# First stage of a two-layer decoder trunk: own buffers for all its loads, issued in a written order, first weights in halves

## Chip, cores and metric

One core of a Trainium2 chip runs the whole program. The metric is device microseconds of one execution; the program of before took 1174.53 us as the median of three runs (1172.65 to 1175.73).

## What is computed

A decoder trunk over 512 tokens of width 1024 with two layers, batch 1, all inputs float32. Layer 0 is a gated DeltaNet mixer beside a cross-attention into 256 memory tokens, layer 1 a sliding-window attention beside the same kind of memory attention; each has a squared-ReLU MLP and layer norms. Cut to what the first stage of the kernel feeds:

```python
def memory_cross_attention(qm, mem, w_kv):      # both layers, mem is an input
    kv = mem @ w_kv
    k = kv[..., :MEM_W]; v = kv[..., MEM_W:]    # MEM_W = 256
    ...

def mixer_a(h, mem, w_in, ...):                 # layer 0, h = x
    proj = h @ w_in
    qkv = proj[..., :c1]
    z = proj[..., c1:c1 + DN_V_W]
    a = proj[..., c1 + DN_V_W:c1 + DN_V_W + DN_HEADS]
    b = proj[..., c1 + DN_V_W + DN_HEADS:c1 + DN_V_W + 2 * DN_HEADS]
    qm = proj[..., c1 + DN_V_W + 2 * DN_HEADS:]
    beta = jax.nn.sigmoid(b); g = -jnp.exp(A_log) * jax.nn.softplus(a + dt_bias)
    o = gated_delta_rule(q, k, v, g, beta)
    ...
```

## The kernel before

Every float32 matrix is split into a high part (a cast to fp32r on ScalarE, ACT) and a low part (the rest, a subtraction on VectorE, DVE), and each product takes three matmuls: high times high, high times low, low times high. `wload` (L81) does this for weights: a raw buffer `wr` of a pool with three of them, one DMA from the queue of SyncE (SP), the cast into `wh` (L87), the subtraction into `wl` (L88); `wh` and `wl` have four buffers each. `split_load` (L192) does it for the transposed activations, with six raw buffers `xr`, in two halves of 256 KB.

The first stage is the memory keys and values of both layers (L205 to L220). `MH` and `ML` are the halves of the memory tokens; for layer i = 0, 1 the values `VM` come first (two weight slabs `wmv`, two groups of 24 matmuls of 256 columns), then the keys `KM` (two slabs `wmk`, two groups of 24 matmuls of 256 columns). So there are 8 groups of 24 matmuls. The second memory block is loaded behind the first weight slab (L210). Then come the loads of the four token blocks of x into `XH` and `XL` (L221), eight small loads (convolution weights, gate constants, positions, L223 to L231), and the stores of the keys and values of layer 1 to DRAM (`kv1`, L232 and L233), from where layer 1 reads them back far later (L1042). The tiles of this stage lie in the pool `mp`, which closes at L234; the pool `dp` of the mixer then takes its place, so a first write to a `dp` tile waits for whatever used that memory.

Behind it stands the first projection, `proj_z(2, ab)` (L255): two slabs of `wz`, four token blocks, 24 matmuls of 260 columns each, 96 in all; it gives the last z columns and the 12 gate columns `ab`. The gates are worked out from `ab` by a chain of small operations on DVE and ACT (L258 to L298). The memory queries `qm` and the keys and queries `kq` of the heads follow on TensorE (PE), by the hand-written list `MIXER_ORDER`.

A scheduler sets the order of each engine's instructions from the program's order and the dependencies; each engine then works strictly in that order. On the SP queue a load into a buffer that is still in use waits there, with all loads behind it. The weight loads use these lines:

```python
    wpool = [None, 3, 4]
        raw = wp.tile(shape, F32, tag="wr", name=nm("wr"), bufs=wpool[1])
        SY.dma_start(raw, src)
        hi = wp.tile(shape, F32R, tag="wh", name=nm("wh"), bufs=wpool[2])
```

Of the kernel before, what the change touches and what calls it, by code (L numbers as in the profile page):

```python
# [11 lines left out]
F32 = mybir.dt.float32  # L12
F32R = mybir.dt.float32r
# [5 lines left out]
P = 128  # L19
S = 512  # L20
D = 1024
NT = S // P
KT = D // P
NH = 6
CW = 260
# [24 lines left out]
def trunk(ctx: ExitStack, tc: tile.TileContext, xT, xn, memT, wk, wq, wv, wqm, wz, wmk, wmv, wo0, wo1, up, dn,  # L50
          bw, ws, conv, alog, dtb, nw, sinks, lng, lnb, lngb, pos, invf, out):
    nc = tc.nc
    V, G, A, T, SY = nc.vector, nc.gpsimd, nc.scalar, nc.tensor, nc.sync
# [8 lines left out]
    def nm(s):  # L62
        uid[0] += 1
        return f"{s}_{uid[0]}"

    def ct(shape, tag, dt=F32):
        return cp.tile(shape, dt, tag=tag, name=tag)

    def mmt(n="mm"):
        return pmm.tile([P, 512], F32, tag="mm", name=nm(n))  # L70

    def smt(n="sm"):
        return psm.tile([P, 512], F32, tag="sm", name=nm(n))

    def fr(ap):
        return ap.bitcast(F32)


    wpool = [None, 3, 4]

    def wload(src, shape):  # L81
        wp = wpool[0]
# [3 lines that stand above are left out]
        lo = wp.tile(shape, F32R, tag="wl", name=nm("wl"), bufs=wpool[2])  # L86
        A.copy(hi, raw)  # L87
        V.tensor_sub(lo, raw, fr(hi))  # L88
        return hi, lo
# [3 lines left out]
    XH = ct([P, KT, S], "XH", F32R)  # L93
    XL = ct([P, KT, S], "XL", F32R)
# [6 lines left out]
    def feature_major(ps, w, mov_hi, mov_lo):  # L101
        hi, lo = w
        for k in range(KT):
            mh, ml = mov_hi(k), mov_lo(k)
            T.matmul(ps, hi[:, k, :], mh, start=(k == 0), stop=False)
            T.matmul(ps, hi[:, k, :], ml, start=False, stop=False)
            T.matmul(ps, lo[:, k, :], mh, start=False, stop=(k == KT - 1))

    def token_major(ps, slabs, st_hi, st_lo):
        nk = sum(h.shape[1] for h, _ in slabs)  # L110
        k = 0
        for hi, lo in slabs:
            for kk in range(hi.shape[1]):
                sh, sl = st_hi(k), st_lo(k)
                T.matmul(ps, sh, hi[:, kk, :], start=(k == 0), stop=False)  # L115
                T.matmul(ps, sh, lo[:, kk, :], start=False, stop=False)  # L116
                T.matmul(ps, sl, hi[:, kk, :], start=False, stop=(k == nk - 1))  # L117
                k += 1
# [19 lines left out]
    def tok(t):  # L138
        return slice(t * P, (t + 1) * P)
# [4 lines left out]
    def x_tok(buf, t):  # L144
        return lambda k: buf[:, k, tok(t)]


    pa = ExitStack()
    km0 = pa.enter_context(tc.tile_pool(name="km0", bufs=1, side="right"))

    def c0(shape, tag, dt=F32):

        return km0.tile(shape, dt, tag=tag, name=tag)
# [31 lines left out]
    mpool = ctx.enter_context(ExitStack())  # L185
    mp = mpool.enter_context(tc.tile_pool(name="mp", bufs=1, side="right"))
    KM = [km0.tile([P, 2, 256], F32, tag="KM0", name="KM0"), mp.tile([P, 2, 256], F32, tag="KM1", name="KM1")]
    VM = [km0.tile([P, 2, 256], F32, tag="VM0", name="VM0"), mp.tile([P, 2, 256], F32, tag="VM1", name="VM1")]
    kv1 = drp.tile([2, P, 512], F32, tag="kv1", name="kv1", bufs=1)
    MH = mp.tile([P, 2, KT, P], F32R, tag="MH", name="MH")  # L190
    ML = mp.tile([P, 2, KT, P], F32R, tag="ML", name="ML")
    def split_load(src, hi, lo):  # L192
        raw = mp.tile([P, KT, P], F32, tag="xr", name=nm("xr"), bufs=6)
        for j in (slice(0, 4), slice(4, 8)):
            SY.dma_start(raw[:, j], src[:, j])
        for j in (slice(0, 4), slice(4, 8)):
            A.copy(hi[:, j], raw[:, j])
            V.tensor_sub(lo[:, j], raw[:, j], fr(hi[:, j]))

    warm_in = mp.tile([P, P], F32, tag="warm_in", name="warm_in")  # L200
    V.memset(warm_in, 1.0)
    warm = smt("warm")
    for i in range(14):
        T.matmul(warm[:, 0:P], warm_in, warm_in, start=True, stop=True)
    split_load(memT[0], MH[:, 0], ML[:, 0])  # L205
    for i in range(2):
        slabs = []
        for kh in range(2):
            slabs.append(wload(wmv[i, kh], [P, 4, 256]))
            if i == 0 and kh == 0:  # L210
                split_load(memT[1], MH[:, 1], ML[:, 1])
        for m in range(2):
            ps = mmt("VM")
            token_major(ps[:, :256], slabs, lambda k: MH[:, m, k, :], lambda k: ML[:, m, k, :])
            A.copy(VM[i][:, m, :], ps[:, :256])
        for j in range(2):
            w = wload(wmk[i, j], [P, KT, P])
            ps = mmt("KM")
            feature_major(ps[:, :256], w, lambda k: MH[:, :, k, :], lambda k: ML[:, :, k, :])
            A.copy(KM[i][:, j, :], ps[:, :256])  # L220
    for t in range(NT):  # L221
        split_load(xT[t], XH[:, :, tok(t)], XL[:, :, tok(t)])
    SY.dma_start(convw, conv)  # L223
    SY.dma_start(gbT, lngb)
    alog_b = row_bcast(alog, NH, "alog_b")
# [3 lines left out]
    invf_b = row_bcast(invf, 32, "invf_b")  # L229
    pos_i = ct([P, NT], "pos_i", I32)  # L230
    SY.dma_start(pos_i, pos)  # L231
    SY.dma_start(kv1[0], KM[1].rearrange("p a b -> p (a b)"))  # L232
    SY.dma_start(kv1[1], VM[1].rearrange("p a b -> p (a b)"))  # L233
    mpool.close()  # L234


    dp = pa.enter_context(tc.tile_pool(name="dp", bufs=2, side="right"))

    def dt_(shape, tag, bufs=2, dt=F32):
        return dp.tile(shape, dt, tag=tag, name=nm(tag), bufs=bufs)  # L240

    def proj_z(zg, gates=None):

        slabs = [wload(wz[zg, kh], [P, 4, CW]) for kh in range(2)]
        c0 = zg * CW
        n = min(CW, 768 - c0)
        for t in range(NT):
            ps = mmt("proj_zMM")
            token_major(ps[:, :CW], slabs, x_tok(XH, t), x_tok(XL, t))
            A.copy(res[:, t, c0:c0 + n], ps[:, :n])  # L250
            if gates is not None:
                V.tensor_copy(gates[:, :, t], ps[:, n:n + 12])

    ab = c0([P, 12, NT], "ab")
    proj_z(2, ab)  # L255


    gg = [c0([P, 24], f"gate{i}") for i in range(12)]  # L258
# [34 lines left out]
    ps = smt("v6ps")  # L293
# [10 lines left out]
    def make_E1(gi):  # L304
        E1 = dt_([P, NU, P], "E1")
        for hl in range(GH):
            h = GH * gi + hl
            ps = smt("E1")
            psv = ps.rearrange("p (c i) -> p c i", c=4)
            for i, eng in enumerate((V, G)):  # L310
                gm = dt_([P, 4, P], "y", dt=F32R)
                eng.tensor_tensor(gm, triu[:, :].unsqueeze(1).broadcast_to([P, 4, P]),
                                  fr(gsp[i])[:, h * 4:h * 4 + 4].unsqueeze(2).broadcast_to([P, 4, P]), op=ALU.mult)
                T.matmul(ps, slow, gm.rearrange("p c i -> p (c i)"), start=(i == 0), stop=(i == 1))
            dst = E1[:, hl * 4:hl * 4 + 4, :]
            V.tensor_tensor(dst, psv, mtri[:, :].unsqueeze(1).broadcast_to([P, 4, P]), op=ALU.add)
            A.activation(dst, dst, AF.Exp)
        E1s[gi] = E1

    def conv_silu(ps, ch, dst):  # L320
        y = dt_([P, 512], "y")
        A.activation(y, ps, AF.Identity, scale=convw[:, ch, 3:4])
        for s in (1, 2, 3):
            V.scalar_tensor_tensor(y[:, s:], ps[:, :512 - s], convw[:, ch, 3 - s:4 - s], y[:, s:],
                                   op0=ALU.mult, op1=ALU.add)
        A.activation(dst, y.rearrange("p (c i) -> p c i", c=4), AF.Silu)
# [415 lines left out]
    def second_pools():  # L742
# [7 lines left out]

    steps = {"E": make_E1, "g": group_open, "k": group_kq, "i": inv_blocks, "j": inv_join, "v": group_v,
             "w": group_v2, "c": group_chunk, "o": chunk_out, "q": proj_qm, "m": mem0, "M": flush, "z": proj_z,
             "n": z_norm, "W": wo_open, "f": close_tile, "p": wo_tile, "X": second_pools, "L": ln_tile}
    run_steps(MIXER_ORDER, steps)
# [281 lines left out]
    with tc.tile_pool(name="l1", bufs=2) as lp:  # L1036
# [155 lines left out]
        slabs = {}  # L1192
# [89 lines left out]
```

## Time and profile before

| | us |
|---|---|
| median of three runs | 1174.53 (1172.65 to 1175.73) |
| the profiled execution, its own time | 1170.9 |
| its span | 1169.2 |
| PE busy | 1137.7 (97%) |
| DVE, ACT, POOL busy | 860.7, 555.8, 242.5 |
| granted clock of PE, mean of the span | 0.992 of full speed |

The span is the profiled execution from its first to its last instruction; 1.7 us lie around it. A granted clock of 1.00 is the level of 2.4 GHz, 0.50 that of 1.2 GHz. Where one engine is busy nearly all the time, the time of the kernel is that engine's work, its rate, and the stretches in which it waits.

### The profile page before, as it was taken

The numbers are of one execution on the slowest core, as the hardware profiler recorded it, in microseconds if no ns is written. First come the engines' busy times: TensorE is split into PE (matmuls) and PEld (weight loads), VectorE is DVE, ScalarE is ACT, GpSimd is POOL, SyncE is SP. The second block draws the span as 40 slices with busy tenths as digits, with TensorE's granted clock in tenths as the row PEclk, the third lists the DMA queues.
The fourth block names the chain that finished last, engine by engine and source line by source line (L and its number), as shares of the span: only waits on it lengthen the run. The fifth ranks groups of instructions, "written<-read, shape, count | busy, mean of one in ns | idle before, by whom it ended". The sixth has DMA issues, their size and how long they took to land.

```text
span 1169.2 us, 18962 instructions
## 1 busy us (share of the span) xinstructions
PE 1137.7 (97%) x7470; PEld 1000.1 (86%) x7470; DVE 860.7 (74%) x1606; ACT 555.8 (48%) x1010; POOL 242.5 (21%) x180
## 2 busy tenths in 40 slices
PE   8999999999999999999999999999999999999996
PEld 8877788879998989898998887778989998989985
DVE  5568899777798666667665968986987666676657
ACT  6345454655385434444443337562655344444431
POOL 1112111101005232423220100000042324242204
PEclk9999999999999999999999999999999999999998
DMA  7522141203413324232332242102333242323311
GB/s 257 194 63 77 61 137 37 68 20 105 166 57 127 124 75 139 76 125 92 100 117 92 71 129 71 54 21 72 109 118 118 77 140 73 126 91 105 112 37 72
DMA packets 40729, 114.16 MB, mean 98 GB/s; under 512 B 11136, under 2 KB 12032, under 8 KB 40640
## 3 DMA queue, kind: packets, MB, share of 16 engines
q1 hardware_dynamic: 40064, 112.04, 29.8%
q8 instruction: 58, 0.95, 0.3%
q10 hardware_dynamic: 576, 0.92, 0.2%
q14 instruction: 31, 0.25, 0.1%
HBM read 109.53 MB, written 3.41 MB: 97 GB/s over the span
## 4 chain that ended last, share of the span: by engine, by line
PE 76%; DVE 15%; ACT 3%; DMA 2%; issue 2%; POOL 1%; POOLq 0%; SPq 0%; ACTq 0%; DVEq 0%
PE dn L116 9%; PE dn L117 9%; PE dn L115 9%; PE upb L884 3%; PE upb L885 3%; PE upb L886 3%; PE wo L117 2%; DVE wl L88 2%; PE wo L115 2%; PE wo L116 2%; PE upd L885 2%; PE upd L884 2%; PE upd L886 2%; PE upa L885 2%; PE upa L884 2%; PE upa L886 2%
## 5 line engine op out<-in xcount | busy, mean ns | idle before, releaser
L87 ACT CAST wh<-wr 128x1024 fp32r<-128x1024 f32 (+1 forms) x136 | 142.6, 1052 | 221.9 <-PE dn L117 154.6
L88 DVE TENSOR_TENSOR wl<-wr,wh 128x1024 fp32r<-128x1024 f32 (+1 forms) x136 | 166.3, 1225 | 77.7 <-ACT wh L87 77.0
L115 PE MATMUL dn<-wh,hh 128*128 128x512 f32 x512 | 199.5, 390 | 0.0
L117 PE MATMUL dn<-wh,hl 128*128 128x512 f32 x512 | 199.4, 389 | 0.0
L116 PE MATMUL dn<-wl,hh 128*128 128x512 f32 x512 | 199.4, 389 | 0.0
L117 PEld LDWEIGHTS dn<-wh,hl 128*128 128x128 f32 x512 | 96.1, 188 | 20.1
L963 DVE TENSOR_TENSOR res<-res,dn 128x512 f32<-128x512 f32 x120 | 81.8, 682 | 42.4 <-PE dn L117 42.3
L116 PEld LDWEIGHTS dn<-wl,hh 128*128 128x128 f32 x512 | 96.1, 188 | 19.1
L115 PEld LDWEIGHTS dn<-wh,hh 128*128 128x128 f32 x512 | 96.1, 188 | 19.0
L874 POOL TENSOR_TENSOR sa<-wr 128x512 f32<-128x512 f32 x26 | 39.0, 1500 | 351.0 <-DMA wr<-in_up_dram 311.1
L662 POOL TENSOR_TENSOR rs<-rs,nhalf 128x1 f32<-128x1 f32 x16 | 13.3, 833 | 327.2 <-DVE rs L661 264.0
L884 PE MATMUL upb<-TH,wh 128*128 128x256 f32 x208 | 57.5, 277 | 1.5 <-DVE u L923 1.5
L885 PE MATMUL upa<-XL,wh 128*128 128x256 f32 x208 | 57.7, 277 | 0.0
L886 PE MATMUL upa<-XH,wl 128*128 128x256 f32 x208 | 57.5, 276 | 0.0
L122 DVE TENSOR_TENSOR hl<-r,hh 128x1024 fp32r<-128x1024 f32 x26 | 56.1, 2156 | 1.9 <-ACT hh L121 1.9
L885 PE MATMUL upb<-TL,wh 128*128 128x256 f32 x208 | 57.4, 276 | 0.0
L886 PE MATMUL upb<-TH,wl 128*128 128x256 f32 x208 | 57.4, 276 | 0.0
L884 PE MATMUL upd<-XH,wh 128*128 128x256 f32 x208 | 57.4, 276 | 0.0
L885 PE MATMUL upd<-XL,wh 128*128 128x256 f32 x208 | 57.4, 276 | 0.0
L886 PE MATMUL upd<-XH,wl 128*128 128x256 f32 x208 | 57.4, 276 | 0.0
L875 POOL TENSOR_TENSOR sb<-sa,wr 128x512 f32<-128x512 f32 x26 | 57.4, 2207 | 0.0
L121 ACT CAST wh<-wr 128x1024 fp32r<-128x1024 f32 x26 | 27.4, 1053 | 53.5 <-PE upa L885 53.5
(405 smaller groups left out, 3296.8 us busy)
## 6 DMA issues: line engine op xcount, KB each, us to landing
wr<-in_up_dram SPq DMA_DIRECT2D x64, 512.0 KB, 4.3
wr<-in_dn_dram SPq DMA_DIRECT2D x64, 512.0 KB, 4.3
wr<-in_wo_dram SPq DMA_DIRECT2D x16, 512.0 KB, 3.6
wr<-in_bw_dram SPq DMA_DIRECT2D x8, 512.0 KB, 4.5
wr<-in_wz_dram SPq DMA_DIRECT2D x6, 520.0 KB, 4.4
wr<-in_wk_dram SPq DMA_DIRECT2D x6, 512.0 KB, 3.6
wr<-in_wq_dram SPq DMA_DIRECT2D x6, 512.0 KB, 3.7
wr<-in_wv_dram SPq DMA_DIRECT2D x6, 512.0 KB, 3.6
```

The source lines that it names most:

```text
L87: A.copy(hi, raw)
L88: V.tensor_sub(lo, raw, fr(hi))
L115: T.matmul(ps, sh, hi[:, kk, :], start=(k == 0), stop=False)
L116: T.matmul(ps, sh, lo[:, kk, :], start=False, stop=False)
L117: T.matmul(ps, sl, hi[:, kk, :], start=False, stop=(k == nk - 1))
L122: return V.tensor_sub(lo, src, fr(hi))
L874: G.tensor_tensor(sa[:, 0], raw[1][:, kA], raw[1][:, kB], op=ALU.add)
L875: G.tensor_tensor(sb[:, 0], sa[:, 0], raw[0][:, kA], op=ALU.subtract)
L884: T.matmul(ps, hi[:, k, :], m, start=start and k == 0, stop=False, skip_group_check=True)
L885: T.matmul(ps, hi[:, k, :], ml[:, k, :], start=False, stop=False, skip_group_check=True)
L886: T.matmul(ps, lo[:, k, :], mh[:, k, :], start=False, stop=stop and k == 3, skip_group_check=True)
L963: V.tensor_tensor(dst, dst, ps, op=ALU.add)
```

## The change

The first stage's loads are taken out of `wload` and `split_load`. `load` makes a raw buffer, a function that issues one piece of it, and a function that splits it piece by piece; `w_load` and `x_load` use it with ten buffers `w0` for weights and six `xr`, all in `mp`. So every load up to and with the two `wz` slabs has its own buffer. All are issued from one list, before any of the work. The two value slabs of layer 0 come in halves of 256 KB, each with its own cast and subtraction. The token block 0 is split before the keys of layer 1, the others behind the casts of the `wz` slabs; the stores of `kv1` and the end of `mp` move behind `proj_z`. Two of the 14 warm-up matmuls go.

```diff
--- before.py
+++ after.py
@@ -189,37 +189,50 @@
     kv1 = drp.tile([2, P, 512], F32, tag="kv1", name="kv1", bufs=1)
     MH = mp.tile([P, 2, KT, P], F32R, tag="MH", name="MH")
     ML = mp.tile([P, 2, KT, P], F32R, tag="ML", name="ML")
-    def split_load(src, hi, lo):
-        raw = mp.tile([P, KT, P], F32, tag="xr", name=nm("xr"), bufs=6)
-        for j in (slice(0, 4), slice(4, 8)):
-            SY.dma_start(raw[:, j], src[:, j])
-        for j in (slice(0, 4), slice(4, 8)):
-            A.copy(hi[:, j], raw[:, j])
-            V.tensor_sub(lo[:, j], raw[:, j], fr(hi[:, j]))
+
+    def load(src, shape, cuts, tag, bufs):
+
+        raw = mp.tile(shape, F32, tag=tag, name=nm(tag), bufs=bufs)
+
+        def piece(i):
+            SY.dma_start(raw[:, cuts[i]], src[:, cuts[i]])
+
+        def split(hi, lo):
+            for j in cuts:
+                A.copy(hi[:, j], raw[:, j])
+                V.tensor_sub(lo[:, j], raw[:, j], fr(hi[:, j]))
+            return hi, lo
+        return piece, split
+
+    def cut(n, parts=2):
+        return [slice(i * n // parts, (i + 1) * n // parts) for i in range(parts)]
+
+    def x_load(src):
+        return load(src, [P, KT, P], cut(KT), "xr", 6)
+
+    def w_load(src, shape, parts=1):
+        piece, split = load(src, shape, cut(shape[1], parts), "w0", 10)
+        wp = wpool[0]
+
+        def halves():
+            return split(*(wp.tile(shape, F32R, tag=t, name=nm(t), bufs=wpool[2]) for t in ("wh", "wl")))
+        return piece, halves
 
     warm_in = mp.tile([P, P], F32, tag="warm_in", name="warm_in")
     V.memset(warm_in, 1.0)
     warm = smt("warm")
-    for i in range(14):
+    for i in range(12):
         T.matmul(warm[:, 0:P], warm_in, warm_in, start=True, stop=True)
-    split_load(memT[0], MH[:, 0], ML[:, 0])
-    for i in range(2):
-        slabs = []
-        for kh in range(2):
-            slabs.append(wload(wmv[i, kh], [P, 4, 256]))
-            if i == 0 and kh == 0:
-                split_load(memT[1], MH[:, 1], ML[:, 1])
-        for m in range(2):
-            ps = mmt("VM")
-            token_major(ps[:, :256], slabs, lambda k: MH[:, m, k, :], lambda k: ML[:, m, k, :])
-            A.copy(VM[i][:, m, :], ps[:, :256])
-        for j in range(2):
-            w = wload(wmk[i, j], [P, KT, P])
-            ps = mmt("KM")
-            feature_major(ps[:, :256], w, lambda k: MH[:, :, k, :], lambda k: ML[:, :, k, :])
-            A.copy(KM[i][:, j, :], ps[:, :256])
-    for t in range(NT):
-        split_load(xT[t], XH[:, :, tok(t)], XL[:, :, tok(t)])
+    mems = [x_load(memT[m]) for m in range(2)]
+    vw = [[w_load(wmv[i, kh], [P, 4, 256], 2 - i) for kh in range(2)] for i in range(2)]
+    kw = [[w_load(wmk[i, j], [P, KT, P]) for j in range(2)] for i in range(2)]
+    xs = [x_load(xT[t]) for t in range(NT)]
+    zw = [w_load(wz[2, kh], [P, 4, CW]) for kh in range(2)]
+    for (piece, _), i in ((mems[0], 0), (vw[0][0], 0), (vw[0][0], 1), (mems[0], 1), (vw[0][1], 0), (vw[0][1], 1),
+                          (mems[1], 0), (mems[1], 1), (kw[0][0], 0), (kw[0][1], 0), (vw[1][0], 0), (vw[1][1], 0),
+                          (xs[0], 0), (xs[0], 1), (kw[1][0], 0), (kw[1][1], 0), (zw[0], 0), (zw[1], 0),
+                          *((x, j) for x in xs[1:] for j in range(2))):
+        piece(i)
     SY.dma_start(convw, conv)
     SY.dma_start(gbT, lngb)
     alog_b = row_bcast(alog, NH, "alog_b")
@@ -229,19 +242,28 @@
     invf_b = row_bcast(invf, 32, "invf_b")
     pos_i = ct([P, NT], "pos_i", I32)
     SY.dma_start(pos_i, pos)
-    SY.dma_start(kv1[0], KM[1].rearrange("p a b -> p (a b)"))
-    SY.dma_start(kv1[1], VM[1].rearrange("p a b -> p (a b)"))
-    mpool.close()
-
-
-    dp = pa.enter_context(tc.tile_pool(name="dp", bufs=2, side="right"))
-
-    def dt_(shape, tag, bufs=2, dt=F32):
-        return dp.tile(shape, dt, tag=tag, name=nm(tag), bufs=bufs)
-
-    def proj_z(zg, gates=None):
-
-        slabs = [wload(wz[zg, kh], [P, 4, CW]) for kh in range(2)]
+    mems[0][1](MH[:, 0], ML[:, 0])
+    for i in range(2):
+        slabs = []
+        for kh in range(2):
+            slabs.append(vw[i][kh][1]())
+        if i == 0:
+            mems[1][1](MH[:, 1], ML[:, 1])
+        for m in range(2):
+            ps = mmt("VM")
+            token_major(ps[:, :256], slabs, lambda k: MH[:, m, k, :], lambda k: ML[:, m, k, :])
+            A.copy(VM[i][:, m, :], ps[:, :256])
+        if i == 1:
+            xs[0][1](XH[:, :, tok(0)], XL[:, :, tok(0)])
+        for j in range(2):
+            w = kw[i][j][1]()
+            ps = mmt("KM")
+            feature_major(ps[:, :256], w, lambda k: MH[:, :, k, :], lambda k: ML[:, :, k, :])
+            A.copy(KM[i][:, j, :], ps[:, :256])
+
+    def proj_z(zg, gates=None, slabs=None):
+
+        slabs = slabs or [wload(wz[zg, kh], [P, 4, CW]) for kh in range(2)]
         c0 = zg * CW
         n = min(CW, 768 - c0)
         for t in range(NT):
@@ -252,7 +274,19 @@
                 V.tensor_copy(gates[:, :, t], ps[:, n:n + 12])
 
     ab = c0([P, 12, NT], "ab")
-    proj_z(2, ab)
+    slabs = [w[1]() for w in zw]
+    for t in range(1, NT):
+        xs[t][1](XH[:, :, tok(t)], XL[:, :, tok(t)])
+    proj_z(2, ab, slabs)
+    SY.dma_start(kv1[0], KM[1].rearrange("p a b -> p (a b)"))
+    SY.dma_start(kv1[1], VM[1].rearrange("p a b -> p (a b)"))
+    mpool.close()
+
+
+    dp = pa.enter_context(tc.tile_pool(name="dp", bufs=2, side="right"))
+
+    def dt_(shape, tag, bufs=2, dt=F32):
+        return dp.tile(shape, dt, tag=tag, name=nm(tag), bufs=bufs)
 
 
     gg = [c0([P, 24], f"gate{i}") for i in range(12)]
```

On the SP queue at the program's start, before (`xr` are activations, `wr` and `w0` weights; a row with x2 is two DMAs):

```order
L195 DMA xr_138<-in_memT_dram 128x512 x2
L84 DMA wr_145<-in_wmv_dram 128x1024
L195 DMA xr_151<-in_memT_dram 128x512 x2
L84 DMA wr_158<-in_wmv_dram 128x1024
L84 DMA wr_216<-in_wmk_dram 128x1024
L84 DMA wr_248<-in_wmk_dram 128x1024
L195 DMA xr_408<-in_xT_dram 128x512 x2
L84 DMA wr_280<-in_wmv_dram 128x1024
```

and in the change, with the semaphores that a row waits for (a DMAHW number is the count of an earlier load):

```order
L198 DMA xr_2_136<-in_memT_dram 128x512
L198 DMA w0_4_138<-in_wmv_dram 128x512 x2
L198 DMA xr_2_136<-in_memT_dram 128x512
L198 DMA w0_5_139<-in_wmv_dram 128x512 x2
L198 DMA xr_3_137<-in_memT_dram 128x512 x2
L198 DMA w0_8_142<-in_wmk_dram 128x1024 [waits DMAHW0_49]
L198 DMA w0_9_143<-in_wmk_dram 128x1024 [waits DMAHW1_49]
L198 DMA w0_6_140<-in_wmv_dram 128x1024 [waits DMAHW2_49]
L198 DMA w0_7_141<-in_wmv_dram 128x1024 [waits DMAHW3_49]
L198 DMA xr_12_146<-in_xT_dram 128x512 [waits DMAHW4_49]
```

The weights of layer 0's values stand as four pieces between the halves of the memory tokens, and the only waits left on the queue here are counts of earlier loads, each for the load eight places before.

On the SP queue where the stage ends, before:

```order
L231 DMA pos_i<-in_pos_dram 128x4
L233 DMA kv_118<-VM_117 128x512
L84 DMA wr_457<-in_wz_dram 128x1040
L84 DMA wr_463<-in_wz_dram 128x1040
L84 DMA wr_635<-in_wqm_dram 128x1024
L232 DMA kv_118<-KM_115 128x512
L84 DMA wr_713<-in_wk_dram 128x1024
```

and in the change:

```order
L244 DMA pos_i<-in_pos_dram 128x4
L282 DMA kv_118<-VM_117 128x512
L281 DMA kv_118<-KM_115 128x512
L84 DMA wr_639<-in_wqm_dram 128x1024
L84 DMA wr_717<-in_wk_dram 128x1024
L84 DMA wr_754<-in_wq_dram 128x1024
```

The `wz` loads are gone from here (they stand far ahead), and the load of `wqm` now stands behind both stores.

On ACT, the casts and copies at the start of the change (MH and wh are the high parts):

```order
L202 CAST MH<-xr_136 128x512 [waits DMAHW0_49]
L202 CAST wh_194<-w_4_138 128x512 [waits DMAHW1_49]
L202 CAST MH<-xr_136 128x512 [waits DMAHW3_49]
L202 CAST wh_194<-w_4_138 128x512 [waits DMAHW2_49]
L202 CAST wh_200<-w_5_139 128x512 [waits DMAHW4_49]
L202 CAST wh_200<-w_5_139 128x512 [waits DMAHW5_49]
L202 CAST MH<-xr_137 128x512 [waits DMAHW6_49]
L202 CAST MH<-xr_137 128x512 [waits DMAHW7_49]
```

The third cast is that of the fourth load: the second half of the first slab is cast behind the second half of the memory block.

## Rows read from the trace of the kernel before

**Rows 1.** The page: busy time of each engine over the span
```profile
PE 1137.7 (97%) x7470; PEld 1000.1 (86%) x7470; DVE 860.7 (74%) x1606; ACT 555.8 (48%) x1010; POOL 242.5 (21%) x180
```
**Rows 2.** Waits of PE from 0 to 60 us: us in total, times, longest
```profile
PE VM L115 <- ACT wh L87: 2.1, 1, 2.1
PE proj_zMM L115 <- ACT wh L87: 1.6, 1, 1.6
...
PE v6ps L294 <- DVE gate L289: 0.4, 1, 0.4
```
**Rows 3.** Timeline of PE in the first stage: start us, us
```profile
1.11 4.86 PE L204 MATMUL warm<-warm_in 128*128 128x128 f32 x28 [1.11 <-DVE warm_in L201]
8.11 0.91 PE L115 MATMUL VM<-wh,MH 128*128 128x256 f32 x2 [2.15 <-ACT wh L87]
9.37 0.38 PE L116 MATMUL VM<-wl,MH 128*128 128x256 f32 x1 [0.35 <-DVE wl L88]
...
14.90 0.28 PE L105 MATMUL KM<-MH,wh 128*128 128x256 f32 x1
```
**Rows 4.** Timeline of PE from the last KM matmul to qm
```profile
31.66 0.28 PE L107 MATMUL KM<-MH,wl 128*128 128x256 f32 x1
33.56 0.63 PE L115 MATMUL proj_zMM<-wh,XH 128*128 128x260 f32 x3 [1.62 <-ACT wh L87]
34.83 0.53 PE L116 MATMUL proj_zMM<-wl,XH 128*128 128x260 f32 x1 [0.65 <-DVE wl L88]
...
35.37 0.42 PE L115 MATMUL proj_zMM<-wh,XH 128*128 128x260 f32 x1
...
37.97 0.42 PE L115 MATMUL proj_zMM<-wh,XH 128*128 128x260 f32 x1
...
43.07 0.28 PE L116 MATMUL proj_zMM<-wl,XH 128*128 128x260 f32 x1
...
46.07 0.28 PE L117 MATMUL proj_zMM<-wh,XL 128*128 128x260 f32 x1
...
47.62 0.39 PE L105 MATMUL qm<-XH,wh 128*128 128x512 f32 x1
```
**Rows 5.** Stretches of 5 us: busy us (instructions) by engine, PE's clock, DMA share, GB/s
```profile
5.00:10.00 5.00, 2.36 (x16) 1.77 (x15) 2.60 (x5) 2.41 (x5) 0.00 (x0) 1.00 0.94 370
...
30.00:35.00 5.00, 2.73 (x22) 2.32 (x21) 1.41 (x2) 2.49 (x3) 0.00 (x0) 0.99 1.02 408
35.00:40.00 5.00, 5.00 (x30) 5.00 (x31) 2.47 (x3) 1.62 (x3) 2.67 (x4) 0.67 0.72 215
```
**Rows 6.** Timeline of SP where the stage ends
```profile
27.58 0.87 SPq L84 DMA_DIRECT2D wr<-in_wz_dram  x2
28.54 0.38 SPq L84 DMA_DIRECT2D wr<-in_wqm_dram  x1
32.37 0.33 SPq L232 DMA_DIRECT2D kv<-KM  x1
```
**Rows 7.** Timeline of ACT in the first stage
```profile
3.49 0.62 ACT L197 CAST MH<-xr 128x512 fp32r<-128x512 f32 x1 [1.42 <-DMA xr<-in_memT_dram]
4.42 0.62 ACT L197 CAST MH<-xr 128x512 fp32r<-128x512 f32 x1 [0.31 <-DMA xr<-in_memT_dram]
7.01 1.04 ACT L87 CAST wh<-wr 128x1024 fp32r<-128x1024 f32 x1 [1.98 <-DMA wr<-in_wmv_dram]
7.96 1.14 ACT L197 CAST MH<-xr 128x512 fp32r<-128x512 f32 x2
9.71 1.05 ACT L87 CAST wh<-wr 128x1024 fp32r<-128x1024 f32 x1 [0.61 <-DMA wr<-in_wmv_dram]
```
**Rows 8.** Timeline of DVE: two subtractions of 256 KB in a row, then two of `wz`
```profile
15.26 1.29 DVE L198 TENSOR_TENSOR XL<-xr,XH 128x512 fp32r<-128x512 f32 x2
...
33.54 2.54 DVE L88 TENSOR_TENSOR wl<-wr,wh 128x1040 fp32r<-128x1040 f32 x2 [5.37 <-ACT wh L87]
```
**Rows 9.** Loads from 0 to 80 us: KB each, median us to landing
```profile
wr<-in_wqm_dram SPq DMA_DIRECT2D x1, 512.0 KB, 7.9
```

## Prediction

> **What bounds the kernel now.** I read the busy times first: PE works in 97% of the span [rows 1], so the time is PE's work, its rate and its waits. Then the waits of PE in the stretch that the change touches: before its real work 2.1 us for the split of the first value slab, later 1.6 us for that of the first `wz` slab, and 0.4 us for the gates [rows 2]. The timeline shows where they lie, with a smaller wait behind each of the first two. The warm-up ends at 5.97 us. At 8.11 come two matmuls, and from 9.37 PE runs without a pause [rows 3] to the last KM matmul, which starts at 31.66 [rows 4] and would be followed by the next at 31.78. From 9.37 to 14.90, where the keys begin, are 46 of the 48 matmuls of the first values: 0.12 us each. So the stage has no starvation between 9.37 and 31.78; it starts late and ends with a hole. In the hole PE waits to 33.56, does three matmuls, waits to 34.83, and then runs slowly: 12 steps from 35.37 to 37.97 are 0.217 us each, against 0.120 for the 25 steps from 43.07 to 46.07 [rows 4]. The granted clock is 0.67 in the stretch from 35 to 40 us [rows 5], the mean of a part at the lower level (1.2 GHz) and a part at the full one (2.4 GHz).
>
> The cause of the hole stands on the SP queue. The two `wz` loads are issued only at 27.58, as third in a chain of buffers that must come free [rows 6]; nothing of PE's work needed that delay.
>
> **The hole before the gate projection.** `proj_z` takes 96 matmuls. At 0.120 us they are 11.5 us, and if they followed the last KM matmul they would end at 31.78 + 11.5 = 43.3; `qm` starts at 47.62 [rows 4]. Closing the hole gives 4.3 us. Its parts: 1.8 us to 33.56, 0.9 us between the three matmuls and 34.83, and the rest, 1.6 us, is the lower clock: at 0.217 - 0.120 = 0.097 us each, some 16 matmuls.
>
> Does the change close it? In its queue the `wz` slabs are loads 17 and 18. With them 6.8 MB must come; that is 18 us at 370 GB/s, a row of this stage [rows 5]. Their casts wait for a free `wh` buffer of four, the last uses being in the values of layer 1, some 7 and 5 us before the last keys end. Two casts of some 1.05 us [rows 7] and two subtractions of 2.54 together [rows 8] then still fit. What is late next would be token blocks 1 to 3, now cast behind these slabs: six casts at 0.52 us steps [rows 7] are 3.1 us, and block 1 is needed only 24 x 0.12 = 2.9 us after `proj_z` starts. So I take the whole 4.3.
>
> **The start.** In the change half a memory block and half a slab come first. The row nearest to these two is the cast of the first two memory halves at 3.49 and 4.42 [rows 7]; so some six matmuls can run from 5.5 us, when the shorter warm-up ends (two of 14 matmuls are 4 of its 28 records, about 0.45 us off 5.97; worth nothing, as PE waits next). ACT's next cast is the second memory half, the fourth load. Call its start T. From there ACT casts every 0.52 us and DVE subtracts every 0.61 [rows 7, 8]: the last of the three weight pieces behind it is split 0.65 + 3 x 0.61 + 0.69 = 3.2 us after T. Then come the last five matmuls of the first group and all 24 of the second: 29 x 0.12 = 3.5. With 0.1 us for handovers the first values end at T + 6.8, against 14.90 now [rows 3].
>
> For T the trace has a row with the same bytes ahead: the first slab of before ends 1.05 MB and its cast starts at 7.01 [rows 7]. The lower end is full rate from the first landing on: three pieces of 262 KB at 408 GB/s [rows 5] are 2.0 us behind 3.49, T = 5.5. The upper end is that loads in flight share the rate and all eight land together: the slab that ends 2.1 MB is cast at 9.71 [rows 7]. I take 7.0, the row with equal bytes: the values end at 13.8, **1.1 us** earlier (2.6 at the lower end, 1.6 later at the upper). Halving the slabs adds two casts and two subtractions, which are in this chain.
>
> By the Trainium skill, DMA: Bandwidth & Descriptors, section Anatomy of one DMA (its fit is for the software path), a DMA takes about 2.0 us and its bytes at 436 GB/s. By it I estimate T = 0.79 + 2.0 + 2.4 = 5.2, 2.9 us gained at the start and 7.2 in all. The trace differs: it has 7.01 for these bytes.
>
> **What is moved.** Ten buffers take the SP waits away, but each load still waits for the one eight places before. The eight small loads are issued behind the big ones, and only the exponential of `alog` stands before a copy that matters; they have some 5 us. The `kv1` stores move from 27.15 and 32.37 to about 31.3 and are read a layer later; the next pool's first tile is written only behind the gates, which start when `proj_z` ends. The `wqm` load was issued at 28.54 and now follows the last store, at about 31.7. Even with the 7.9 us that it took before [rows 9] it is there at 39.6 and cast at 40.7, while `proj_z` ends at 30.7 + 11.5 = 42.2: covered by 1.5 us.
>
> **The sum.** 4.3 + 1.1 = 5.4 us. Behind the gates each engine's order is that of before, and every wait there counts from `ab`, so the head start stays. The profiled execution took 1170.9 us: 1165.5. The median of the three runs is 3.6 us above that execution, so the forecast is 1174.5 - 5.4 = **1169.1 us**. A measurement of this kernel can tell 0.3%, 3.5 us, from no change.
>
> **Rivals.**
> *Full rate at once.* The early loads land as at 408 GB/s, T = 5.5. For it: more loads in flight from the start, none waiting for a buffer. Against: 7.01 in the trace. Gain 4.3 + 2.6 = 6.9, 1167.6.
> *Loads share the rate.* T = 9.7, gain 4.3 - 1.6 = 2.7, 1171.8, within 0.3%. For it: the first slab's cast comes 2.6 us behind the second half's [rows 7], twice what 524 KB need at 408 GB/s, with later loads in flight. Against: the first two halves were cast 0.93 us apart in their order.
> *The clock falls once in the starved start.* PE does some six matmuls, then waits for pieces. The trace shows both outcomes: two matmuls between 5.97 and 9.37 [rows 3] and the granted clock stayed at 1.00 [rows 5]; three between 31.78 and 34.83 and it fell, at a price of 1.6 us [rows 4, 5]. Gain 3.8, 1170.7. TensorE: Matmul & The Clock Gate of the Trainium skill, section HAM oscillation, says that bursts of matmuls between DMA waits run each at the lower clock. The first hole in the trace speaks against this as a certainty, the second for it as a risk.
> *Slower: the clock stays down through the start.* If it is not up when the pieces trickle in, each matmul costs 0.097 us more. From 56 such matmuls the 5.4 us are gone, from 92 it is slower by 0.3%; with all 192 of the memory stage it is 18.6 - 5.4 = 13 us, 1187.7. Against: after the hole in the trace full work brought the clock back within some 16 matmuls.
> *The gain is lost behind.* `wqm` lands late, since it now queues behind two stores. From 9.4 us to landing PE waits; at 12 to 15 us all but 0 to 3 us of the gain is gone, 1171.7 to 1174.5. The longest landing of a weight in this stage is 7.9 us [rows 9].
> *The change does not free the queue*, because of the count of eight: the `wz` slabs would come too late only if the 6.8 MB took to 28 us, below 273 GB/s; no stretch read here with loads waiting is so slow over its length.
>
> **Chances.** Forecast 0.50, full rate 0.17, shared rate 0.10, one fall of the clock 0.11, lost behind (with the queue) 0.08, clock down 0.04. Over 0.3% faster are the first two and a part of the shared rate and of the one fall: 0.75. Within: 0.20. Slower: 0.05. The range reaches from the full rate less 2 us of spread between runs (the three lie 3.1 us apart) to the shared rate with 1.2 us added: 1165.6 to 1173.0.
>
> **What would show it.** Right: `wz` issued before 20 us, no wait of PE between KM and `proj_z`, clock at 1.00 from 30 to 40 us, KM starting at 13.8, `qm` at 42.2 instead of 47.62, and the same 5 us or so at the end. Wrong at the start: KM begins at 12.3 or 16.5. Wrong behind: a wait of PE for `wh` of `wqm`, or for the gates of more than the 0.4 us of before. Wrong altogether: a granted clock near 0.5 between 8 and 20 us.

## The result, and the profile after

The changed kernel took 1164.25 us (median of four runs, 1162.93 to 1167.8) against 1175.05 us for the kernel before (four runs): a ratio of 0.9918, with a 95% interval of 0.9895 to 0.9941. That is faster, as forecast, and by about twice the forecast 5.4 us. Three later comparisons with more runs of before gave less:

| comparison | changed, us (runs) | before, us (runs) | ratio, 95% interval |
|---|---|---|---|
| first | 1164.25 (4) | 1175.05 (4) | 0.9918 (0.9895 to 0.9941) |
| second | 1164.26 (6) | 1171.93 (23) | 0.9937 (0.9920 to 0.9955) |
| third | 1165.53 (4) | 1172.44 (18) | 0.9938 (0.9921 to 0.9956) |
| fourth | 1165.68 (4) | 1172.44 (18) | 0.9941 (0.9925 to 0.9957) |

The kernel before, compared with itself three times (e8, e9, e11 below), came out at 1.0011, 1.0011 and 1.0004, so 0.001, about 1 us, is not to be read from such a ratio. I take the gain to be 7 us, 0.6%: more than the 5.4 us of the sum, less than the 9.6 us (0.0082 of 1171 us) of the first comparison.

The page of after, against [rows 1]; then the longest waits of PE from 0 to 60 us, against [rows 2]:

```profile
PE 1132.5 (98%) x7466; PEld 995.5 (86%) x7466; DVE 858.9 (74%) x1608; ACT 555.5 (48%) x1012; POOL 241.6 (21%) x180
```
```profile
PE VM L115 <- ACT wh L202: 1.7, 1, 1.7
...
PE v6ps L328 <- DVE gate L323: 0.3, 1, 0.3
```

The wait for the first `wz` slab is gone. The timeline of PE, against [rows 3, 4]:

```profile
5.82 0.36 PE L115 MATMUL VM<-wh,MH 128*128 128x256 f32 x1
...
8.44 0.38 PE L115 MATMUL VM<-wh,MH 128*128 128x256 f32 x1 [1.69 <-ACT wh L202]
9.25 0.38 PE L116 MATMUL VM<-wl,MH 128*128 128x256 f32 x1 [0.42 <-DVE wl L203]
...
14.23 0.28 PE L105 MATMUL KM<-MH,wh 128*128 128x256 f32 x1
...
31.07 0.28 PE L115 MATMUL proj_zMM<-wh,XH 128*128 128x260 f32 x1
...
42.55 0.40 PE L105 MATMUL qm<-XH,wh 128*128 128x512 f32 x1
```

`proj_z` follows the last keys at 31.07 without a pause, and `qm` starts at 42.55 instead of 47.62: 5.07 us earlier. The stretches of 5 us, against [rows 5], show the clock up where it had fallen:

```profile
30.00:35.00 5.00, 5.00 (x44) 5.00 (x43) 1.55 (x4) 0.80 (x3) 0.92 (x2) 1.00 0.49 153
35.00:40.00 5.00, 5.00 (x44) 5.00 (x43) 2.54 (x3) 2.49 (x4) 2.74 (x4) 1.00 0.70 254
```

On SP the loads run ahead, and the `wqm` load stands behind the second store, against [rows 6]:

```profile
11.37 1.59 SPq L198 DMA_DIRECT2D w<-in_wz_dram  x2
...
31.67 0.33 SPq L281 DMA_DIRECT2D kv<-KM  x1
32.05 0.42 SPq L84 DMA_DIRECT2D wr<-in_wqm_dram  x1
```

And on ACT, against [rows 7], the third row is T, the cast of the second memory half, and the last is that of `wqm`:

```profile
3.60 0.62 ACT L202 CAST MH<-xr 128x512 fp32r<-128x512 f32 x1 [1.53 <-DMA xr<-in_memT_dram]
4.31 0.62 ACT L202 CAST wh<-w 128x512 fp32r<-128x512 f32 x1
7.25 0.62 ACT L202 CAST MH<-xr 128x512 fp32r<-128x512 f32 x1 [2.32 <-DMA xr<-in_memT_dram]
...
35.79 1.05 ACT L87 CAST wh<-wr 128x1024 fp32r<-128x1024 f32 x1 [1.29 <-DMA wr<-in_wqm_dram]
```

So the first stage did nearly what the sum says. But the span fell by 1169.2 - 1161.1 = 8.1 us, and 5.07 of it are there at `qm`. The other 3.0 us came later, in work whose instructions and order on PE are the same in both kernels. The stretches around 215 and 255 us show them; first those of before:

```profile
210.00:220.00 10.00, 8.07 (x34) 6.28 (x33) 9.86 (x21) 6.25 (x14) 1.85 (x1) 0.83 0.17 52
250.00:260.00 10.00, 8.42 (x73) 7.95 (x73) 6.86 (x13) 4.70 (x13) 0.00 (x0) 0.83 0.01 2
```

and the same of after:

```profile
210.00:220.00 10.00, 9.63 (x74) 8.81 (x75) 8.22 (x20) 7.41 (x19) 0.00 (x0) 1.00 0.57 175
250.00:260.00 10.00, 8.79 (x70) 7.89 (x68) 6.35 (x22) 6.71 (x28) 1.70 (x2) 1.00 0.00 1
```

The granted clock fell twice in before, to 0.83 in the mean of 10 us, and not in after. (A fall, from here on, is a stretch in which it is 0.50. Every profile of both kernels has one more in its last 10 us, which is not counted.) The wait at the first place is the same: PE waits for the values `vt` before a transpose, 1.93 us in before and 1.85 us in after. In before:

```profile
215.50 0.84 PE L396 MATMUL vt<-ident,vt 128*128 128x128 f32 x4 [1.93 <-ACT vt L326]
```

and in after:

```profile
210.37 0.66 PE L430 MATMUL vt<-ident,vt 128*128 128x128 f32 x4 [1.85 <-ACT vt L360]
```

Two matmuls behind it, the same two in both kernels, tell where the lead of the changed kernel grows. In before:

```profile
253.36 1.65 PE L490 MATMUL ks<-S,kq 128*128 128x128 f32 x6
...
257.72 0.49 PE L513 MATMUL od<-LT,E 128*128 128x128 f32 x2 [0.46 <-ACT LT L500]
```

and in after:

```profile
246.79 0.94 PE L524 MATMUL ks<-S,kq 128*128 128x128 f32 x6
...
249.63 0.49 PE L547 MATMUL od<-LT,E 128*128 128x128 f32 x2 [0.46 <-ACT LT L534]
```

The lead is 5.07 us at `qm`, 6.57 us at `ks`, behind the first fall, and 8.09 us at `od`, behind the second: 1.5 us for each.

So theory A: what goes beyond the first stage is PE's clock, which falls at such places in one execution and not in another. Its rivals: something behind the gates became shorter for good (B); the halves at the start bring the extra (C); the falls belong to a place in time since the start (D); the kernel before has two of them each time (E).

### The profile page after: what moved, and what is told of

Read it like the earlier page. It is cut to its first block, busy times and chain, and to the rows that moved or that the text cites. A ratio compares the mean times of both kernels' runs of the same rounds, so it can differ in the third digit from the quotient of the medians.

```text
span 1161.1 us, 18955 instructions
## 1 busy us (share of the span) xinstructions
PE 1132.5 (98%) x7466; PEld 995.5 (86%) x7466; DVE 858.9 (74%) x1608; ACT 555.5 (48%) x1012; POOL 241.6 (21%) x180
## 4 chain that ended last, share of the span: by engine, by line
PE 79%; DVE 14%; ACT 3%; issue 2%; POOL 1%; DMA 1%; SPq 0%; POOLq 0%; ACTq 0%; DVEq 0%
PE dn L116 9%; PE dn L115 9%; PE dn L117 9%; PE upb L918 3%; PE upb L920 3%; PE upb L919 3%; PE wo L115 2%; PE wo L117 2%; PE wo L116 2%; PE upd L920 2%; PE upd L919 2%; PE upd L918 2%; PE upa L919 2%; PE upa L918 2%; PE upa L920 2%; DVE y L358 2%
## 5 line engine op out<-in xcount | busy, mean ns | idle before, releaser
L87 ACT CAST wh<-wr 128x1024 fp32r<-128x1024 f32 (+1 forms) x126 | 132.2, 1052 | 216.4 <-PE dn L117 155.2
L88 DVE TENSOR_TENSOR wl<-wr,wh 128x1024 fp32r<-128x1024 f32 (+1 forms) x126 | 154.0, 1224 | 65.8 <-ACT wh L87 65.3
```

## Experiments

**The changed kernel again (e1).** No edit.

> The changed kernel once more, so that its spread is known. Both theories: PE begins the keys near 14.2 us and qm near 42.6 us in the profile, 5.1 us ahead of the kernel before. Theory A (what goes beyond these 5.1 us is PE's clock, which falls to 1.2 GHz at some short waits of the mixer in one execution and not in another): the runs differ by steps of some 1.7 us, span and granted clock move together (0.0015 of the clock for each fall), and the mean gain over the kernel before is 5 us plus 1.7 us for each fall more in the runs of before, so between 5 and 11 us. Theory B (something in the work behind the gates became shorter for good): all runs gain 8 to 11 us at equal granted clock.

Measured: 1164.26 us (1161.89 to 1166.99), ratio 0.9937 (0.9920 to 0.9955). Its six runs go from 1161.89 at a granted clock of 0.998 to 1166.99 at 0.995; the 23 runs of before beside it from 1168.15 at 0.996 to 1175.01 at 0.990. This profile of the same program has a fall at the start (the stretch, the first KM matmul, and `qm`):

```profile
10.00:15.00 5.00, 5.00 (x33) 5.00 (x33) 2.51 (x5) 2.94 (x5) 1.23 (x2) 0.70 1.02 414
```
```profile
15.58 0.28 PE L105 MATMUL KM<-MH,wh 128*128 128x256 f32 x1
...
43.91 0.40 PE L105 MATMUL qm<-XH,wh 128*128 128x512 f32 x1
```

The keys come 1.35 us later than in the first profile, and one more fall stands near 250 us. Both theories had the keys near 14.2 us, so this fall was in neither; from keys to `qm` it is 28.3 us, as in the first profile. Time and clock move together, as A has it. B wanted 8 to 11 us at equal clock. Over all comparisons here the clock is on record for 98 runs of before and 18 of the changed kernel. At 0.996 are nine of before, with 1167.9 to 1169.4 us, and six of the changed kernel, with 1162.9 to 1165.0: 4.4 us less in the mean. At 0.995 it is 3.4 us and at 0.994 5.1. B falls, and some 4 of the 7 us are there without any difference of the clock.

**The hole closed, the start as before (e2).**

```diff
-    for i in range(12):
+    for i in range(14):
...
-    vw = [[w_load(wmv[i, kh], [P, 4, 256], 2 - i) for kh in range(2)] for i in range(2)]
+    vw = [[w_load(wmv[i, kh], [P, 4, 256], 1) for kh in range(2)] for i in range(2)]
...
-    for (piece, _), i in ((mems[0], 0), (vw[0][0], 0), (vw[0][0], 1), (mems[0], 1), ...
+    for (piece, _), i in ((mems[0], 0), (mems[0], 1), (vw[0][0], 0), (mems[1], 0), (mems[1], 1), (vw[0][1], 0), ...
```

The second memory block is split behind the first slab, as before.

> The changed kernel with the start of before: memory blocks first, value slabs whole, 14 warm-up matmuls, everything else as changed. The keys begin at 14.9 us instead of 14.2, no hole before proj_z, qm at 43.3 us. Theory A: 0.7 us slower than the changed kernel with equal falls of the clock, 4.3 us faster than before, plus or minus the falls behind the gates. Rival C (the start in halves is what brings the extra gain): 1169 us or more, no faster than 5 us over before.

Measured: 1166.98 us, ratio 0.9955 (0.9939 to 0.9970), 5.3 us faster than before by the ratio and 2.1 slower than e1. In its profile the clock fell at the start, with the keys at 15.82 us and `qm` at 44.14: from keys to `qm` 28.3 us, as in the changed kernel. It fell once more near 250 us. The hole is most of the gain. Rival C expected 1169 us or more, and the time is 2 us below that; C's other bound, a gain of at most 5 us, lies inside the interval (3.5 to 7.1). The difference to e1 is larger than the 0.7 us expected, and the two intervals are too wide to tell 0.7 from 2.1.

**The start alone, the hole as before (e3).**

```diff
-    zw = [w_load(wz[2, kh], [P, 4, CW]) for kh in range(2)]
...
-                          (xs[0], 0), (xs[0], 1), (kw[1][0], 0), (kw[1][1], 0), (zw[0], 0), (zw[1], 0),
+                          (xs[0], 0), (xs[0], 1), (kw[1][0], 0), (kw[1][1], 0),
...
-    slabs = [w[1]() for w in zw]
...
-    proj_z(2, ab, slabs)
+    proj_z(2, ab)
```

> The changed kernel with the wz slabs loaded by wload again, behind the small loads. The keys begin near 14.2 us, the wz loads are issued near 27.5 us, PE waits 1.5 to 3 us between the last keys and proj_z, and its clock may fall there. Theory A: 0.7 us faster than before if the clock falls in the hole, up to 2.5 us if it does not, plus or minus falls behind the gates. Theory B or C: it keeps the 3 to 5 us that are not explained by the hole, 1168 to 1171 us.

Measured: 1169.22 us, ratio 0.9972 (0.9961 to 0.9983), 3.3 us faster than before (2.0 to 4.6). That is above theory A's range of 0.7 to 2.5 us and inside the 3 to 5 us, and the 1168 to 1171 us, that B and C expected: this run alone does not speak for A. With e2 it puts the start at 2.1 (e1 against e2) to 3.3 us, more than the 0.7 us by which the keys came earlier. Its twelve runs span 1164.86 us at a clock of 0.998 to 1170.83 us at 0.993: one program, 6 us, and the clock goes with them. The profile has the keys at 14.03, the hole with its fall, `qm` at 46.48, and another fall near 185 us, where no other profile so far had one.

It also shows what the hole hangs on. The `wz` loads found free buffers and were issued at 25.13 us, 2.4 us earlier than in before and than expected, right behind the small loads. They had landed by 30.8 us (4.3 and 5.2 us after their issues). Still PE waited 1.42 and 0.65 us, because ACT had their casts behind the copy of the last keys, for which it idled 2.50 us:

```profile
31.05 0.37 ACT L261 COPY KM<-KM 128x256 f32<-128x256 f32 x1 [2.50 <-PE KM L107]
31.32 2.02 ACT L87 CAST wh<-wr 128x1040 fp32r<-128x1040 f32 x2
```

In the first profile of the changed kernel both casts stand before that copy:

```profile
24.26 1.06 ACT L202 CAST wh<-w 128x1040 fp32r<-128x1040 f32 x1 [1.04 <-PE VM L117]
...
26.01 1.07 ACT L202 CAST wh<-w 128x1040 fp32r<-128x1040 f32 x1
```

So free buffers and a somewhat earlier load do not close the hole; the place of the casts in ACT's order belongs to it.

**The changed kernel, shifted (e4).**

```diff
-    for i in range(12):
+    for i in range(47):
         T.matmul(warm[:, 0:P], warm_in, warm_in, start=True, stop=True)
```

> The changed kernel with 47 warm-up matmuls instead of 12: the whole rest is shifted by some 5 us, qm comes near 47.6 us as in the kernel before, without the hole and with the clock up. Theory A: falls of the clock behind the gates come by chance, so 5 us slower than the changed kernel, near 1169 us, with a granted clock as in that kernel. Rival D (the falls belong to places in time since the start, so that a kernel whose gates come at 47.6 us has them and one at 42.6 us has not): two falls come back as in the profile of before, 8 to 10 us slower than the changed kernel, 1172 to 1174 us, the falls near 216 and 253 us.

Measured: 1169.31 us, 5.05 us slower than e1, with a clock of 0.9945 in the mean of twelve runs (e1 0.9955). `qm` came at 47.98, where before has it, and the two falls did not come back: there is none near 216, and one long one from 248 to 258 us, which covers the second of D's places. Rival D, that wanted both falls and 8 to 10 us, falls.

**The wait at the start of before filled (e5).**

```diff
-    for i in range(14):
+    for i in range(24):
```

> The kernel before with 24 warm-up matmuls instead of 14, so that PE works on until the first slab is split near 8.1 us. Theory A1 (in some executions of before the clock falls in the wait from 6.0 to 9.4 us, and that is part of what the changed start removed): faster by 0.5 to 1.4 us, with a granted clock higher by 0.0005 to 0.0013. Rival (the clock does not fall there in before): within 0.3 us of before.

Measured: ratio 1.0018 (1.0007 to 1.0028) to before; before against itself in the same comparison (e8) had 1.0011. So no gain, and the 0.5 to 1.4 us that A1 expected did not come; with 1.0011 taken off it is 0.8 us slower, which does not matter here. The profile tells why a better start alone can be worth nothing there: the keys came at 14.69 us without a fall, and the wait before `proj_z` grew to 3.43 us, because the `wz` load was issued no earlier than before (at 27.44 us) and came in later (6.9 us after its issue against 5.2):

```profile
35.16 1.02 PE L115 MATMUL proj_zMM<-wh,XH 128*128 128x260 f32 x3 [3.43 <-ACT wh L87]
```

Its clock then fell in the hole, near 190 us and for long near 255 us, so that its span of 1173.0 us does not show what the start is worth.

**The hole of before filled with work (e6).** Thirteen matmuls on a constant tile go into the tile that `proj_z` then overwrites.

```diff
             ps = mmt("proj_zMM")
+            for _ in range(13 if gates is not None and t == 0 else 0):
+                T.matmul(ps[:, 0:P], ones, ones, start=True, stop=True)
             token_major(ps[:, :CW], slabs, x_tok(XH, t), x_tok(XL, t))
```

> The kernel before with 13 matmuls on a constant tile in the wait between the last keys and proj_z; they write the tile that proj_z overwrites. The wait for the wz slab stays, the clock should stay up. Theory A: the fall of the clock is 1.6 us of the 4.3 us of the hole, so 1.2 to 1.6 us faster than before, granted clock higher by 0.0014. Rival (the clock falls there anyway, or does not matter as something else is late): no change.

Measured: 1169.67 us, ratio 0.9991 (0.9980 to 1.0002). The median lies 2.3 us under that of before, and all eleven runs (1167.4 to 1170.9) lie under the ten of before in e8, of the same comparison (1171.7 to 1174.7); the paired ratio says 1 us, with no change inside its interval. So it looks faster, as theory A has it, by an amount that is not decided. The granted clock, 0.9945 in the mean, is 0.0017 above that of the 27 runs of before; 0.0014 was expected. In the profile the clock stayed up through the hole:

```profile
35.00:40.00 5.00, 4.55 (x40) 4.34 (x39) 3.38 (x3) 2.70 (x3) 1.21 (x2) 1.00 0.74 257
```

It fell at the start, with the keys at 17.20 us, and once near 255 us.

**The start of the changed kernel filled (e7).** The matmuls go on the warm-up's tile, between two matmuls of the first group of values alone.

```diff
                 sh, sl = st_hi(k), st_lo(k)
+                for _ in range(9 if fill and k == 2 else 0):
+                    behind(T.matmul(fill[0][:, 0:P], fill[1], fill[1], start=True, stop=True), last)
...
```

`behind` keeps them behind the sixth matmul in PE's order.

> The changed kernel with 9 matmuls of the warm-up kind between the sixth and the seventh matmul of the first values, where PE waits near 7 us. Theory A: the fall of the clock in the start, seen in the profile of the changed kernel's second run and not in its first, is gone: the mean is 0.5 to 1.4 us below the changed kernel, near 1163.5 us, and the keys begin near 14.2 us in every profile. Rival (the fall at the start is rare): within 0.3 us of the changed kernel.

Measured: 1164.39 us, ratio 0.9941 (0.9927 to 0.9955), no better than the changed kernel's 0.9937 to 0.9941. The profile had no fall anywhere before its last 10 us, and the keys at 14.63. The 0.5 to 1.4 us that A expected do not show: by the ratio it does not beat the changed kernel by anything that can be measured, which is what the rival had. One profile does not tell whether the fall at the start is gone.

**More profiles of both kernels (e8 to e12).** No edits.

> The kernel before under a profile once more. Theory A: the clock falls in the hole at 35 us again; behind the gates and at the start its falls stand elsewhere than in the first profile (then 216 and 253 us, none at the start). Rival D: they stand at the same places.

> The kernel before, third profile: which falls of the clock belong to it? Theory A (falls come by chance at places where PE waits or does little): one in the hole at 35 us, one at the start in about two of three profiles (it puts the keys near 17 us instead of 14.9), and between none and two behind the gates. The time from the start of qm to the end is 1118.2 us plus 1.5 to 1.8 us for each fall behind the gates. Rival E (the kernel before has two falls behind the gates each time, near 216 and 255 us): two again.

> The changed kernel, third profile. Theory A: keys at 14.2 us without and 15.6 us with a fall at the start, qm at 42.6 or 43.9 us, between none and two falls behind the gates, and from qm to the end 1118.2 us plus 1.5 to 1.8 us for each. Rival E: at most one fall behind the gates each time.

> As the third profile of the kernel before: a fourth one, for the count of falls. Theory A: none to two behind the gates; rival E: two at the same places.

> As the third profile of the changed kernel: a fourth one, for the count of falls. Theory A: none to two behind the gates; rival E: at most one. Over both pairs the changed kernel is 6.5 to 8.5 us faster.

All eight profiles of the two kernels, cut at the start of the first KM matmul and of `qm` (us; span minus `qm` is the rest):

| kernel, profile | to KM | KM to qm | qm to end | span | falls: start, hole, behind |
|---|---|---|---|---|---|
| before, first | 14.90 | 32.72 | 1121.6 | 1169.2 | 0, 1, 2 |
| before, e8 | 16.98 | 32.51 | 1121.9 | 1171.4 | 1, 1, 2 |
| before, e9 | 14.68 | 33.29 | 1118.8 | 1166.8 | 0, 1, 0 |
| before, e11 | 17.71 | 31.13 | 1122.1 | 1170.9 | 1, 0, 1 long |
| changed, first | 14.23 | 28.32 | 1118.6 | 1161.1 | 0, 0, 0 |
| changed, e1 | 15.58 | 28.33 | 1119.5 | 1163.4 | 1, 0, 1 |
| changed, e10 | 15.76 | 28.33 | 1120.3 | 1164.4 | 1, 0, 1 |
| changed, e12 | 15.78 | 28.32 | 1120.6 | 1164.7 | 1, 0, 1 |

The profile e9 of before refutes rival E: no fall behind the gates, and its rest, 1118.8 us, is that of the first profile of the changed kernel. The wait of PE in its hole, and `qm`; then two stretches behind the gates, with the clock up:

```profile
34.16 0.63 PE L115 MATMUL proj_zMM<-wh,XH 128*128 128x260 f32 x3 [2.45 <-ACT wh L87]
...
47.97 0.39 PE L105 MATMUL qm<-XH,wh 128*128 128x512 f32 x1
```
```profile
215.00:220.00 5.00, 4.16 (x29) 3.53 (x29) 4.97 (x13) 4.78 (x11) 0.00 (x0) 1.00 0.35 105
250.00:255.00 5.00, 4.07 (x48) 3.68 (x46) 4.31 (x9) 1.85 (x7) 0.00 (x0) 1.00 0.01 3
```

The second profile, e8, had not told them apart: contrary to what I expected of A, its falls behind the gates stood at the same two places as in the first. And in e11, also of before, the clock was down in the start, and in the hole, which had two waits of 1.42 and 0.65 us, it did not fall; in e8 and e3, with the same two waits, it did:

```profile
10.00:15.00 5.00, 5.00 (x24) 5.00 (x25) 3.91 (x6) 3.14 (x3) 2.03 (x3) 0.50 0.87 293
35.00:40.00 5.00, 3.19 (x23) 2.90 (x24) 3.50 (x3) 3.22 (x4) 1.34 (x2) 1.00 0.68 235
```

The price of a fall behind the gates: three profiles without one have a rest of 1117.9 (e7), 1118.6 and 1118.8 us; six with one short one (e1, e2, e3, e6, e10, e12) have 1119.4 to 1120.6, in the mean 1120.0. That is 1.5 us each, as expected ahead of e9; two cost 3.2 to 3.5 us, and a long one 2.6 (e4) and 3.7 us (e11), which is more than was expected for one. By their ratios e10 and e12 gain 7.3 and 6.9 us, inside the 6.5 to 8.5 expected; the profiles alone, 2.4 and 6.2 us for the two pairs, are too few for that.

## Why the prediction was wrong

Its mechanisms in the first stage were right and are shown: the hole before `proj_z` closes, the start comes forward a little, the head start at `qm` was forecast as 5.4 us and was 5.07 us in the first pair of profiles. The time fell outside the range, because the sum ended at `qm` and the step from there to the median was wrong twice. The profiled execution was forecast as 1165.5 us and took 1162.93, 2.6 less; the median was forecast 3.6 us above it and came 1.3 us above it, 2.3 less. Together that is the 4.9 us between 1169.1 and 1164.25.

- *The hole, 4.3 us: right in size, its cause told in part.* From keys to `qm` before takes 31.1 to 33.3 us and the changed kernel 28.3 each time; 4.1 us in the mean of four profiles each. With the fall in the hole it is 4.2 to 5.0, without it (e11) 2.8. I laid the hole to the late issue of the `wz` loads alone; e3 shows that their casts must also stand before the copy of the last keys on ACT, which the change had done as well.
- *The start, 1.1 us: right in kind, a little too large.* T was 7.25 instead of 7.0, and the values ended 7.0 us after it instead of 6.8; the keys began at 14.23 instead of 13.8, so 0.7 us were gained; over four profiles each it is 0.7 us too. The runs of e2 and e3 put the start at 2.1 to 3.3 us, and what brings the rest is not shown. By the Trainium skill's page (DMA: Bandwidth & Descriptors, Anatomy of one DMA) my estimate for T was 5.2 us; the trace of before, with 7.01, was the better guide.
- *The clock at the start.* I gave one fall a chance of 0.11, in the changed kernel alone. It fell there in three of its four profiles and in two of four of before, where the keys came 2 to 3 us later (in part because the first slab was split later) against 1.4 to 1.6. So it is nearly even between the kernels, and much more common than I had it. The section HAM oscillation of TensorE: Matmul & The Clock Gate (the Trainium skill) has a kernel whose bursts run at the lower clock after each DMA wait of some 3 to 5 us. The waits before the first values were shorter here, 1.1 to 2.4 us at the longest, and the clock fell in five of eight profiles and not in all.
- *"Behind the gates each engine's order is that of before, and every wait there counts from `ab`, so the head start stays": the step that failed.* The waits did stay nearly the same (1.93 and 1.85 us for `vt`), but the time from `qm` to the end is no constant of the program: it goes from 1118.6 to 1122.1 us in eight profiles, for the greater part by the falls of the clock. In the first pair that was 3.0 us for the changed kernel; over four pairs it is 1.4 us in the mean. I had read the lower clock in the hole and not asked where else in the span it was below 1.00; two stretches at 0.83 stood there.
- *The step from the profiled execution to the median.* I added 3.6 us as if they were fixed; this failed too. For the greater part they go with the clock: before has runs of 1168 to 1169 us at 0.996 and of 1171 to 1176 at 0.992. The first comparison had four of the slower ones, so the base of the forecast, 1174.5, was 2.1 to 2.6 us above the medians measured later with 18 to 27 runs.
- *`wqm` covered by 1.5 us: right.* It landed in 3.7 us, was cast at 35.79, and PE did not wait.

What stays open is whether the changed kernel has fewer falls behind the gates for a reason. Before had two, two, none and a long one, the changed kernel none, one, one, one; the mean clock of 23 runs of before is 0.9924 and of six of e1 0.9955, and of all 98 and 18 runs 0.9924 and 0.9954, so there is a difference beyond chance. By my estimate the hole accounts for about a third of it (3 of 4 profiles, 1.6 us of 1170). Where the rest lies, eight profiles do not tell. A shift in time alone does not bring the two falls of before back (e4).

## What to carry to other kernels

Issue the loads of a first stage from one list, each with its own buffer, so that a slab needed at the end of the stage does not wait for buffers that its middle frees, and place its cast before any copy that waits for PE's last work of the stage: here the two together closed a hole of 4 us, and buffers with a load 2.4 us earlier did not (e3). What each alone is worth was not tried. A hole in front of PE costs its length and, here in three of four profiles, a fall of the clock behind it; list every stretch with a granted clock under 1.00 over the whole span before taking one execution as the base of a sum, and take several profiles where the question is below 1%. A better start can be lost again in a later wait that is set by something else, as the profile of e5 shows.

## What the runs showed that I had not expected

The same wait of PE, 1.9 us for `vt`, was followed by a fall of the clock in one execution and not in another, of the same program too (1.93 us in the first profile of before, 1.92 us in e9). But the falls behind the gates do not stand just anywhere: over the fourteen profiles of both kernels and their variants they begin at three places of the work only, some 138 us behind the start of `qm` (e3, e5), 168 us (first profile of before, e8) and 200 to 206 us (ten of the fourteen), each in some executions. A long wait is not even needed: near 185 us (e3) PE was marked busy throughout, for the most part with small matmuls of 32 and 64 columns, when the clock fell to 0.50. And the falls differ in length: from 250 to 255 and 255 to 260 us the granted clock is 0.50 and 0.66 in e4, 0.56 and 0.76 in e11, but 0.80 and 1.00 in e1. One program's runs spread over 6 us (e3), with the clock from 0.998 to 0.993.
